# The opening of a two-layer decoder trunk: its first loads in 128 KB pieces, its first products in program order, and four matmuls of ones

## The chip, the cores and the metric

The kernel runs on one core of one Trainium2 chip. The metric is the device time of one execution in microseconds; the time before the change is 1127.63 us, the median of three runs (1126.76 to 1127.94). One further execution was recorded by the hardware profiler. Five engines work side by side, each through its own list of instructions in order: PE (TensorE: matmuls, with its weight loads shown as PEld), DVE (VectorE), ACT (ScalarE), POOL (GpSimd) and SP (SyncE), which here only issues DMAs.

## The reference

A trunk of two layers over 256 tokens of width 2048, in float32. Each layer normalises, projects, mixes tokens (layer 0: a gated linear recurrence beside an RG-LRU; layer 1: mLSTM), projects back, and then adds a gated embedding of its own:

```python
for i in range(DEPTH):
    hn = rmsnorm(h, e_norm[j] if i % 2 == 0 else o_norm[j])
    ...
    h = h + mix
    pl = rmsnorm(p[i].astype(h.dtype) @ ple_w[i], ple_norm[i])
    h = h + jax.nn.sigmoid(h @ ple_gate_w[i]) * pl
return rmsnorm(h, final_norm)
```

The change touches how `p[0] @ ple_w[0]` is started (a 256x256 matrix by a 256x2048 matrix). Nothing that is computed changes.

## The kernel before

**Numbers in two parts.** Every float32 operand of a large product is split into `hi` (the value rounded to a shorter float, type fp32r) and `lo` (what is left). A product is then three matmuls, hi x hi, hi x lo and lo x hi, summed in PSUM. So each weight that arrives from memory goes through two instructions: ACT writes `whi` (line 123), DVE subtracts and writes `wlo` (line 124). Activations go the same way (`split_act`, lines 138 and 139, tile `ahl`).

**Loading.** `load_weights` (lines 112 to 127) loads one block of 128 x 2048 weights (1 MB) as two halves of 512 KB into tiles `raw` (five buffers), `whi` and `wlo` (four buffers each). With `pieces=2` the first half comes as two transfers of 256 KB, each split as soon as it is there. All loads are issued by SP in program order. The splits are given a high priority (line 122), so the scheduler, which decides each engine's order when the program is built, places them early.

**The opening.** `load_p(0)` (line 321) loads the embedding input, 256 KB, as `praw` and splits it. `ple(0, ...)` (lines 326 to 345) then computes the embedding products: two blocks `b` of weights, four output tiles `j` in each, and for each tile two columns `jj` and two depths `k`. Each (jj, k) is one `mm3` (lines 142 to 145): hi x hi on line 143, hi x lo on line 144, lo x hi on line 145. That is 2 x 4 x 2 x 2 x 3 = 96 matmuls of 256 columns. Tiles j = 0 and 1 use the first half of the block's weights, j = 2 and 3 the second half. The results are copied out of PSUM by ACT (line 343) and DVE (line 341) in turn. The scheduler may interleave these matmuls between tiles as it likes.

**What follows.** The value projection `i_proj` (line 603) runs `project_tok` (lines 176 to 196) twice, 96 matmuls of 512 columns each time (lines 191 to 193). During the first, `load_x` (line 436) brings in the four pieces of `x`; DVE multiplies them by the norm gains (line 302, tile `hn`) and splits them, ACT squares them, and POOL adds the squares (line 285). When the sums are complete, `normed` (line 287) makes the normalised activations on DVE (line 292, again tile `hn`, then the split on lines 138 and 139). The first projection `f_proj` (line 521, matmuls on lines 154 and 160) needs all of them.

The instruction lists below are those of the programs as built.

Of the kernel before, what the change touches and what calls it, by code (L numbers as in the profile page):

```python
# [11 lines left out]
F32 = mybir.dt.float32  # L12
# [4 lines left out]
ALU = mybir.AluOpType  # L17
PSUM = bass.MemoryType.PSUM

P = 128  # L20
T = 256
# [24 lines left out]
def trunk(ctx: ExitStack, tc: tile.TileContext, a, out):  # L46
    nc = tc.nc
    v, s, gp, te, sy = nc.vector, nc.scalar, nc.gpsimd, nc.tensor, nc.sync
# [7 lines left out]
    px = ctx.enter_context(tc.tile_pool(name="px", bufs=3, space=PSUM))  # L56
# [5 lines left out]
    last = {}  # L62
# [27 lines left out]
    ones = cp.tile([P, T], F32, name="ones")  # L90
    gp.memset(ones, 1.0)
    eps = cp.tile([P, 1], F32, name="eps")
    gp.memset(eps, EPS)
    ident = cst[:, 0:128]
    c0 = 128
    lmask = {}
# [7 lines left out]
    def pc(name, i=0, n=None):  # L104
        o, w = PRM[name]
        return prm[:, o + i:o + i + (n or 1)]

    def pall(name):
        return pc(name, 0, PRM[name][1])


    def load_weights(src, pieces=1):
        parts = []
        for hf in range(2):
            raw = wp.tile([P, 1024], F32, name="raw", tag="raw", bufs=5)
            hi = wp.tile([P, 1024], F32R, name="whi", tag="whi")
            lo = wp.tile([P, 1024], F32R, name="wlo", tag="wlo")
            n = 1024 // pieces
            for c in range(0, 1024, n):
                r, h, l = (x[:, c:c + n] for x in (raw, hi, lo))  # L120
                sy.dma_start(out=r, in_=src[:, hf * 1024 + c:hf * 1024 + c + n])
                with tc.high_priority(offset=400):
                    last["act"] = s.copy(h, r).ins  # L123
                    last["dve"] = v.tensor_tensor(out=l, in0=r, in1=h.bitcast(F32), op=ALU.subtract).ins  # L124
            parts.append((hi, lo))
            pieces = 1
        return parts

    def act_pair():

        x = ap.tile([P, 1024], F32R, name="ahl", tag="ahl")
        x4 = x.rearrange("p (k i t) -> p k i t", i=2, k=2)
        return x4[:, :, 0], x4[:, :, 1], x

    def split_act(src, name):
        hi, lo, both = act_pair()
        src = src.rearrange("p (k t) -> p k t", k=2)
        s.copy(hi, src)  # L138
        v.tensor_tensor(out=lo, in0=src, in1=hi.bitcast(F32), op=ALU.subtract)  # L139
        return hi, lo, both  # L140

    def mm3(o, whi, wlo, x, k, first, end):
        te.matmul(o, whi, x[0][:, k], start=first, stop=False)  # L143
        te.matmul(o, whi, x[1][:, k], start=False, stop=False)  # L144
        last["pe"] = te.matmul(o, wlo, x[0][:, k], start=False, stop=end).ins  # L145

    def block(w, act):


        ps = pm.tile([P, 512], F32, name="mm", tag="mm")  # L150
        parts = load_weights(w)
        for k in range(KT):
            c = (k % 8) * P
            last["pe"] = te.matmul(ps, parts[k // 8][0][:, c:c + P],  # L154
                                   act[k // 2][2][:, (k % 2) * 512:(k % 2 + 1) * 512],
                                   start=(k == 0), stop=False).ins
        pump()
        for k in range(KT):
            c = (k % 8) * P
            last["pe"] = te.matmul(ps[:, T:2 * T], parts[k // 8][1][:, c:c + P], act[k // 2][0][:, k % 2],  # L160
                                   start=False, stop=(k == KT - 1)).ins
        return ps
# [6 lines left out]
    def project(w, pair, act, which=(0, 1)):  # L169

        m = tp.tile([P, 512], F32, name="mg", tag="hn", bufs=3)
        for j in which:
            merge(m[:, j * T:(j + 1) * T], block(w[2 * pair + j], act))
        return m

    def project_tok(w, j, act, before=None):

        ps = [pm.tile([P, 512], F32, name="mm", tag="mm") for _ in range(2)]
        for kq in range(4):
            if before is not None:  # L180
                before(kq)
            parts = load_weights(w[4 * j + kq])
            for hf in range(2):
                for kk in range(4):
                    k = kq * 4 + kk
                    hi, lo = parts[kk // 2]
                    c = (kk % 2) * 512
                    ah, al, _ = act[k // 2]
                    xh, xl = (x[:, k % 2, hf * P:(hf + 1) * P] for x in (ah, al))
                    wh, wl = hi[:, c:c + 512], lo[:, c:c + 512]  # L190
                    te.matmul(ps[hf], xh, wh, start=(k == 0), stop=False)  # L191
                    te.matmul(ps[hf], xh, wl, start=False, stop=False)  # L192
                    last["pe"] = te.matmul(ps[hf], xl, wh, start=False, stop=(k == KT - 1)).ins  # L193
                if hf == 0:
                    pump()
        return ps
# [123 lines left out]

    def load_p(i):
        praw = tp.tile([P, 512], F32, name="praw", tag="hn", bufs=3)
        sy.dma_start(out=praw, in_=a["pT"][i])
        return split_act(praw, "p")

    def ple(i, pact, pool, tag, between=None):
        pls = []
        for b in range(2):
            parts = load_weights(a["pw"][2 * i + b], 2 if i == b == 0 else 1)
            if b == 1 and between is not None:  # L330
                between()
            for j in range(4):
                hi, lo = parts[j // 2]
                pl = pool.tile([P, 512], F32, name="pl", tag=tag, bufs=10 if tag == "qk" else 8)
                ps = pm.tile([P, 512], F32, name="mm", tag="mm")
                for jj in range(2):
                    for k in range(2):
                        c = ((j % 2) * 4 + jj * 2 + k) * P
                        mm3(ps[:, jj * T:(jj + 1) * T], hi[:, c:c + P], lo[:, c:c + P], pact, k, k == 0, k == 1)
                if j % 2:  # L340
                    v.tensor_copy(pl, ps)
                else:
                    s.copy(pl, ps)
                pls.append(pl)
        return pls
# [76 lines left out]
    def small(n, name, rows=P):  # L422
        return cp.tile([rows, n], F32, name=name)
# [5 lines left out]
    m0_scope = ExitStack()  # L429
    m0 = m0_scope.enter_context(tc.tile_pool(name="m0", bufs=2))  # L430
    pls = ple(0, load_p(0), p0, "pl", lambda: sy.dma_start(out=prm, in_=a["prm"]))
    identr = cp.tile([8, 8], F32R, name="identr")
    acc = cp.tile([P, 512], F32, name="acc", tag="acc")
# [12 lines left out]
    pgh = []  # L446
    for i in range(2):
        t = small(16, f"pgh{i}")
        v.tensor_scalar(t, pall(f"pn{i}"), 0.5, None, op0=ALU.mult)
        pgh.append(t)  # L450

    norm = {}
# [1 line left out]
    def finish_norm(accs, hq, g, act, lag):  # L454
# [10 lines left out]
    act = []  # L465

    mx, e0, e1, lb, omb, sp, ez, z2, pol, sp8, spm8, anh = (small(8, n) for n in (
        "mx", "e0", "e1", "lb", "omb", "sp", "ez", "z2", "pol", "sp8", "spm8", "anh"))
# [41 lines left out]
    with m0_scope:  # L510
        ew = a["ew"]
        fs, qs, ks = [], [], []
        for g in range(2):
            f = m0.tile([P, 1024], F32, name="f", tag="f")
            k = m0.tile([P, 1024], F32, name="k", tag="k")
            q = m0.tile([P, 1024], F32, name="q", tag="q")
# [209 lines left out]
    for i in range(4):  # L726
        t = hp.tile([P, 1024], F32, name="hq", tag="h")
# [7 lines left out]
    act = []  # L735
# [3 lines left out]
    with tc.tile_pool(name="m1", bufs=2) as m1:  # L739
# [31 lines left out]
        ps = pm.tile([P, 512], F32, name="mm", tag="mm")  # L771
        for hf in range(2):
# [4 lines left out]
            for w in range(2):  # L777
                src = gr[:, hf * 8:(hf + 1) * 8, w * 8:(w + 1) * 8]
                c = w * 32
                s.copy(w3[:, :, c:c + 8], src)  # L780
                v.tensor_tensor(out=w3[:, :, 64 + c:72 + c], in0=src, in1=f3[:, :, c:c + 8], op=ALU.subtract)
            for kk in range(8):
                k = hf * 8 + kk
                for i, x in enumerate(act[k // 2][0:2]):
                    te.matmul(ps[:, 0:T], wt[:, kk * P:(kk + 1) * P], x[:, k % 2],  # L785
                              start=(k == i == 0), stop=(k == KT - 1 and i == 1))
# [131 lines left out]
        for j in range(8):  # L918
            ps = project(a["oog"], j, act)
# [5 lines left out]
            if j >= 3:  # L925
                for jj, t in held:
                    v.scalar_tensor_tensor(nums[jj], t, 1.0, nums[jj], op0=ALU.add, op1=ALU.mult)
                held = []
        pact = load_p(1)
        y = []  # L930
        for j in range(8):
            y.append(gate_split(a["oz"], j, lambda: nums[j], False))

        pls = ple(1, pact, m1, "qk")
        start("pl", ple_norm(1, pls))
        acc = cp.tile([P, 512], F32, name="acc", tag="acc")
        _, accs = finish_layer(hq, a["oo"], a["g1"], y, pls, acc, None)
# [3 lines left out]
        for k, n in ((0, 1), (1, 1), (12, 2), (2, 2), (4, 2), (14, 2), (6, 2), (8, 2), (10, 2)):  # L941
            hh = hq[k // 4][:, (k % 4) * T:(k % 4 + n) * T]
            eng, r = (gp, rs) if k >= 12 else (v, rsp)
# [105 lines left out]
```

## Time and profile before

| | |
|---|---|
| time, median of 3 runs | 1127.63 us (1126.76 to 1127.94) |
| the profiled execution | 1128.09 us |
| its span, first to last instruction | 1126.3 us |
| PE busy | 1098.4 us, 98% of the span |
| DVE busy | 807.5 us, 72% |
| ACT busy | 591.6 us, 53% |
| mean granted TensorE clock | 0.992 |

Times in the views are microseconds from the first instruction of the span. A row of the timeline gives start, duration, engine, line, operation, the tile written and the tiles read, the shape, the number of instructions merged, and in brackets how long the engine had been idle and what ended the idle time. SPq is SP's DMA queue: such a row is the issue of a transfer, not the transfer. A row of the table by windows gives for each stretch the busy time of each engine with its number of instructions, then the granted clock of TensorE, the busy share of the DMA engines, and GB/s.

### The profile page before, as it was taken

To read this page: it belongs to the slowest core of one execution; us is meant where nothing else is said; L and a number is where in the kernel's file an instruction comes from. 1 tells how busy PE (TensorE), PEld (TensorE's weight loads), DVE (VectorE), ACT (ScalarE), POOL (GpSimd) and SP (SyncE) were. 2 spreads that over 40 slices of the span, in tenths; PEclk is the share of its full clock that TensorE was granted. 3 is DMA by queue.
4 is the path that set the end of the run, shared out by engine and by line. 5 is a ranking of instruction groups with operands and counts; after the bars stand their busy time and mean duration, and the time that the engine had idled before them with its cause. 6 is when DMAs were issued, how large, how long until landed. Compare 5 with 4: busy or idle time off the path is not lost.

```text
span 1126.3 us, 16575 instructions
## 1 busy us (share of the span) xinstructions
PE 1098.4 (98%) x6298; PEld 953.9 (85%) x6298; DVE 807.5 (72%) x1197; ACT 591.6 (53%) x812; POOL 110.0 (10%) x80
## 2 busy tenths in 40 slices
PE   7999999999999999999999999999999989999995
PEld 6778898888888888888888888888888888888884
DVE  7998776798867656787745876659566568856775
ACT  6565435666645435555545655544455465435552
POOL 2144000000000000111000011110000013500111
PEclk9999999999999999999999999999999999999997
DMA  8655545443565555555555544444565555555642
GB/s 318 206 177 187 164 138 167 150 150 132 169 205 198 195 187 187 187 188 188 190 188 169 188 135 143 150 149 157 190 203 188 190 168 166 194 189 188 194 137 75
DMA packets 55519, 198.34 MB, mean 176 GB/s; under 512 B 6160, under 2 KB 6672, under 8 KB 55440
## 3 DMA queue, kind: packets, MB, share of 16 engines
q1 hardware_dynamic: 54864, 195.20, 52.2%
q0 software_dynamic: 576, 2.10, 0.6%
q8 instruction: 49, 0.80, 0.3%
q14 instruction: 30, 0.25, 0.1%
HBM read 195.17 MB, written 2.10 MB: 175 GB/s over the span
## 4 chain that ended last, share of the span: by engine, by line
PE 91%; DVE 1%; ACT 1%; issue 0%; POOL 0%; DVEq 0%; ACTq 0%; POOLq 0%
PE mm L154 49%; PE mm L160 26%; PE mm L191 2%; PE mm L193 2%; PE mm L192 2%; PE mx L572 2%; PE mx L875 1%; PE mx L670 1%; PE mm L143 0%; PE mm L144 0%; PE mx L264 0%; PE mm L145 0%; PE st L831 0%; PE mm L785 0%; PE st L631 0%
## 5 line engine op out<-in xcount | busy, mean ns | idle before, releaser
L124 DVE TENSOR_TENSOR wlo<-raw,whi 128x1024 fp32r<-128x1024 f32 (+1 forms) x361 | 456.7, 1300 | 205.0 <-issue 80.1
L154 PE MATMUL mm<-ahl,whi 128*128 128x512 f32 x2432 | 582.5, 392 | 2.3 <-DVE ahl L139 2.3
L123 ACT CAST whi<-raw 128x1024 fp32r<-128x1024 f32 (+1 forms) x361 | 376.5, 1046 | 296.1 <-PE mm L154 224.9
L154 PEld LDWEIGHTS mm<-ahl,whi 128*128 128x128 f32 x2432 | 446.7, 188 | 91.4 <-DVE ahl L139 4.4
L160 PE MATMUL mm<-ahl,wlo 128*128 128x256 f32 x2432 | 322.0, 286 | 0.0
L160 PEld LDWEIGHTS mm<-ahl,wlo 128*128 128x128 f32 x2432 | 310.7, 192 | 11.4 <-issue 1.3
L166 ACT COPY sm<-mm 128x256 f32<-128x256 f32 x120 | 44.4, 371 | 100.4 <-PE mm L160 100.0
L191 PE MATMUL mm<-whi,ahl 128*128 128x512 f32 x192 | 75.6, 394 | 0.1
L193 PE MATMUL mm<-whi,ahl 128*128 128x512 f32 x192 | 74.9, 391 | 0.2 <-DVE ahl L139 0.2
L192 PE MATMUL mm<-wlo,ahl 128*128 128x512 f32 x192 | 75.0, 390 | 0.0
L285 POOL TENSOR_TENSOR acc<-acc,sq 128x512 f32<-128x512 f32 x17 | 27.7, 1628 | 298.1 <-ACT sq L284 223.2
L167 DVE TENSOR_TENSOR mg<-mm,sm 128x256 f32<-128x256 f32 x120 | 50.0, 417 | 2.6 <-ACT sm L166 2.5
L193 PEld LDWEIGHTS mm<-whi,ahl 128*128 128x128 f32 x192 | 36.0, 188 | 8.4 <-DVE ahl L139 1.0
L191 PEld LDWEIGHTS mm<-whi,ahl 128*128 128x128 f32 x192 | 36.1, 188 | 8.1 <-ACT ahl L138 0.5
L192 PEld LDWEIGHTS mm<-wlo,ahl 128*128 128x128 f32 x192 | 36.1, 188 | 7.8 <-DVE wlo L124 0.5
L285 POOL TENSOR_TENSOR placc<-placc,sq 128x512 f32<-128x512 f32 x14 | 22.8, 1625 | 202.0 <-ACT sq L284 176.6
L365 POOL TENSOR_TENSOR pl<-pl,plrs 128x512 f32<-128x512 f32 x16 | 30.9, 1963 | 34.9 <-ACT plrs L276 34.9
L143 PE MATMUL mm<-ahl,whi 128*128 128x256 f32 x64 | 20.0, 313 | 10.8 <-ACT whi L123 7.7
L752 DVE SCALAR_TENSOR_TENSOR qk<-mg,prm,qk 128x255 f32<-128x255 f32 (+2 forms) x48 | 22.2, 479 | 11.6 <-ACT qk L749 11.0
L138 ACT CAST ahl<-hn 128x512 fp32r<-128x512 f32 x32 | 19.4, 616 | 15.9 <-DVE hn L292 9.9
L728 POOL DMA_DIRECT2D hq<-in_xT_dram x4 | 2.3, 578 | 235.1 <-PE mx L624 177.6
L143 PEld LDWEIGHTS mm<-ahl,whi 128*128 128x128 f32 x64 | 13.8, 216 | 11.3 <-ACT whi L123 8.0
(241 smaller groups left out, 777.5 us busy)
## 6 DMA issues: line engine op xcount, KB each, us to landing
raw<-in_ew_dram SPq DMA_DIRECT2D x80, 512.0 KB, 4.4
raw<-in_g_dram SPq DMA_DIRECT2D x64, 512.0 KB, 4.4
raw<-in_eo_dram SPq DMA_DIRECT2D x32, 512.0 KB, 4.8
raw<-in_ov_dram SPq DMA_DIRECT2D x32, 512.0 KB, 4.1
raw<-in_oqk_dram SPq DMA_DIRECT2D x32, 512.0 KB, 4.3
raw<-in_oog_dram SPq DMA_DIRECT2D x32, 512.0 KB, 4.2
raw<-in_oz_dram SPq DMA_DIRECT2D x32, 512.0 KB, 4.3
raw<-in_oo_dram SPq DMA_DIRECT2D x32, 512.0 KB, 4.3
```

Source lines behind the costliest of these rows:

```text
L123: last["act"] = s.copy(h, r).ins
L124: last["dve"] = v.tensor_tensor(out=l, in0=r, in1=h.bitcast(F32), op=ALU.subtract).ins
L143: te.matmul(o, whi, x[0][:, k], start=first, stop=False)
L154: last["pe"] = te.matmul(ps, parts[k // 8][0][:, c:c + P], act[k // 2][2][:, (k % 2) * 512:(k % 2 + 1) * 512], start=(k == 0), stop=False).ins
L160: last["pe"] = te.matmul(ps[:, T:2 * T], parts[k // 8][1][:, c:c + P], act[k // 2][0][:, k % 2], start=False, stop=(k == KT - 1)).ins
L166: s.copy(small, ps[:, T:2 * T])
L167: v.tensor_tensor(out=dst, in0=ps[:, 0:T], in1=small, op=ALU.add)
L191: te.matmul(ps[hf], xh, wh, start=(k == 0), stop=False)
L192: te.matmul(ps[hf], xh, wl, start=False, stop=False)
L193: last["pe"] = te.matmul(ps[hf], xl, wh, start=False, stop=(k == KT - 1)).ins
L285: eng.tensor_tensor(out=acc, in0=acc, in1=sq, op=ALU.add)
L365: gp.tensor_tensor(out=x3, in0=x3, in1=rs.unsqueeze(1).to_broadcast([P, 2, T]), op=ALU.mult)
```

## The change

- A PSUM tile `idle` is taken, and four float32 matmuls of ones by ones (128 x 256) are written into it before anything else; nothing reads it.
- `load_p(0)` loads its input as two transfers of 128 KB, the first issued by SP, the second by ACT, and splits each by itself.
- The first half of the first weight block comes in four pieces of 128 KB instead of two of 256 KB. The splits of these pieces and of the input are chained with `issue_after`, so ACT and DVE take them in this order: input part 0, weight piece 0, input part 1, weight pieces 1, 2, 3. Other weights keep the high priority.
- In `ple`, each `mm3` is chained behind the last PE instruction, so PE takes the embedding products in program order.
- The two small products `pgh` are chained behind the last DVE split.

```diff
+    idle = px.tile([P, 512], F32, name="mx", tag="mx")
+    for _ in range(4):
+        last["pe"] = te.matmul(idle[:, 0:T], ones[:, 0:P], ones, start=True, stop=True).ins
...
+    opening = []
...
-                with tc.high_priority(offset=400):
+                with ExitStack() as order:
+                    if pieces > 1:
+                        for ins in (last["act"], last["dve"]):
+                            order.enter_context(tc.issue_after(ins))
+                    else:
+                        order.enter_context(tc.high_priority(offset=400))
                     last["act"] = s.copy(h, r).ins
                     last["dve"] = v.tensor_tensor(out=l, in0=r, in1=h.bitcast(F32), op=ALU.subtract).ins
+                if opening:
+                    opening.pop()()
...
         praw = tp.tile([P, 512], F32, name="praw", tag="hn", bufs=3)
-        sy.dma_start(out=praw, in_=a["pT"][i])
-        return split_act(praw, "p")
+        if i:
+            sy.dma_start(out=praw, in_=a["pT"][i])
+            return split_act(praw, "p")
+        x = act_pair()
+
+        def part(k):
+            r = praw[:, k * T:(k + 1) * T]
+            with ExitStack() as order:
+                if k:
+                    for ins in (last["act"], last["dve"]):
+                        order.enter_context(tc.issue_after(ins))
+                last["act"] = s.copy(x[0][:, k], r).ins
+                last["dve"] = v.tensor_tensor(out=x[1][:, k], in0=r, in1=x[0][:, k].bitcast(F32),
+                                              op=ALU.subtract).ins
+
+        for k, q in enumerate((sy, s)):
+            q.dma_start(out=praw[:, k * T:(k + 1) * T], in_=a["pT"][i][:, k * T:(k + 1) * T])
+        part(0)
+        opening.append(lambda: part(1))
+        return x
...
-            parts = load_weights(a["pw"][2 * i + b], 2 if i == b == 0 else 1)
+            parts = load_weights(a["pw"][2 * i + b], 4 if i == b == 0 else 1)
...
-                        mm3(ps[:, jj * T:(jj + 1) * T], hi[:, c:c + P], lo[:, c:c + P], pact, k, k == 0, k == 1)
+                        with ExitStack() as behind:
+                            if "pe" in last:
+                                behind.enter_context(tc.issue_after(last["pe"]))
+                            mm3(ps[:, jj * T:(jj + 1) * T], hi[:, c:c + P], lo[:, c:c + P], pact, k, k == 0, k == 1)
...
-        v.tensor_scalar(t, pall(f"pn{i}"), 0.5, None, op0=ALU.mult)
+        with tc.issue_after(last["dve"]):
+            v.tensor_scalar(t, pall(f"pn{i}"), 0.5, None, op0=ALU.mult)
```

## The prediction

> **What bounds the kernel now.** I read four views: the page's engine line and chain, for the whole; the table by windows, for the first 75 us, the only stretch whose built order of instructions the change moves (PE's list is the same from its 334th instruction on, DVE's from its 151st); the timeline of the opening; and the timeline of PE's waits. The page first: busy time of each engine, and the chain of work that ended last by engine.
>
> ```profile
> PE 1098.4 (98%) x6298; PEld 953.9 (85%) x6298; DVE 807.5 (72%) x1197; ACT 591.6 (53%) x812; POOL 110.0 (10%) x80
> ...
> PE 91%; DVE 1%; ACT 1%; issue 0%; POOL 0%; DVEq 0%; ACTq 0%; POOLq 0%
> ```
>
> Over the whole span PE is the bound. That is an average. The windows tell another story for the start (stretch; busy time and count of PE, PEld, DVE, ACT, POOL; clock, DMA share, GB/s):
>
> ```profile
> 6.00:10.20 4.20, 2.45 (x9) 2.16 (x10) 1.39 (x2) 1.75 (x3) 0.00 (x0) 1.00 0.99 350
> 10.20:30.00 19.80, 19.65 (x124) 17.89 (x124) 19.59 (x27) 14.50 (x22) 8.31 (x5) 1.00 0.91 353
> 30.00:50.00 20.00, 19.83 (x88) 15.51 (x87) 19.83 (x69) 12.34 (x20) 1.34 (x2) 1.00 0.61 205
> 50.00:66.00 16.00, 16.00 (x72) 13.28 (x71) 15.51 (x27) 10.10 (x15) 0.00 (x0) 1.00 0.60 197
> 66.00:74.40 8.40, 6.06 (x24) 4.36 (x24) 8.40 (x8) 6.68 (x11) 4.23 (x3) 0.95 0.45 142
> ```
>
> From 10.2 to 74.4 us DVE is busy 19.59 + 19.83 + 15.51 + 8.40 = 63.3 of 64.2 us: it has no slack at all. PE is as full until 66 us and then idles. What it idles for:
>
> ```profile
> 71.61 0.73 PE L154 MATMUL mm<-ahl,whi 128*128 128x512 f32 x2 [1.33 <-DVE ahl L139]
> 73.35 1.12 PE L154 MATMUL mm<-ahl,whi 128*128 128x512 f32 x2 [1.01 <-DVE ahl L139]
> ```
>
> At 70.3 us (71.61 less 1.33) PE has caught up with DVE and waits for the last normalised activations. So in the first 75 us PE runs on time that DVE sets, and the question of this change is when DVE's unbroken stretch begins. The opening:
>
> ```profile
> 0.74 1.28 ACT L138 ACT_TABLE_LOAD   x1 [0.74 <-PEq L1040]
> 0.74 0.31 POOL L91 MEMSET ones<- 128x256 f32 x1 [0.29 <-POOLq L1040]
> 0.74 0.38 SPq L323 DMA_DIRECT2D praw<-in_pT_dram  x1
> ...
> 1.18 2.32 SPq L121 DMA_DIRECT2D raw<-in_pw_dram  x5
> 3.47 0.62 ACT L138 CAST ahl<-praw 128x512 fp32r<-128x512 f32 x1 [1.45 <-DMA praw<-in_pT_dram]
> ...
> 5.49 0.62 ACT L123 CAST whi<-raw 128x512 fp32r<-128x512 f32 x1 [1.40 <-DMA raw<-in_pw_dram]
> ...
> 6.16 0.58 PE L143 MATMUL mm<-ahl,whi 128*128 128x256 f32 x1 [6.16 <-ACT whi L123]
> ...
> 7.88 0.62 ACT L123 CAST whi<-raw 128x512 fp32r<-128x512 f32 x1 [1.77 <-DMA raw<-in_pw_dram]
> ...
> 8.55 0.58 PE L143 MATMUL mm<-ahl,whi 128*128 128x256 f32 x1 [1.59 <-ACT whi L123]
> ...
> 9.17 1.04 ACT L123 CAST whi<-raw 128x1024 fp32r<-128x1024 f32 x1 [0.68 <-DMA raw<-in_pw_dram]
> ...
> 10.25 2.51 DVE L124 TENSOR_TENSOR wlo<-raw,whi 128x1024 fp32r<-128x1024 f32 x2 [1.03 <-ACT whi L123]
> ```
>
> DVE's stretch begins at 10.25 with the split of the block's second half (call it H), behind ACT's cast at 9.17, behind H's landing. The two 256 KB pieces came at 5.49 and 7.88.
>
> **The change part by part.** The sum is made against the profiled execution, 1128.09 us (span 1126.3, so 1.8 us lie around it); the median of the runs, 1127.63, is 0.46 lower.
>
> *Four matmuls of ones.* A float32 matmul of 256 columns is two records; the trace has one at half clock and one at full:
>
> ```profile
> 47.89 0.60 PE L248 MATMUL st<-dg,ones 128*128 128x256 f32 x2
> ...
> 1116.01 1.19 PE L248 MATMUL st<-dg,ones 128*128 128x256 f32 x2 [2.09 <-DVE dg L245]
> ```
>
> They can start when the ones are written, 0.74 + 0.31 = 1.05. Four take between 4 x 0.60 = 2.4 and 4 x 1.19 = 4.8 us; nothing has run before, so I take the upper end: until 5.8 at most. Today's first weights are cast at 5.49, so they can hold up the first product by 0.3 us, which (below) has cover. Cost 0.
>
> *The loads.* SP's issues stand 2.32 / 5 = 0.46 us apart. H is today the third of the five, issued at 1.18 + 2 x 0.46 = 2.1; afterwards the input's part and four pieces stand before it: 0.74 + 0.44 + 4 x 0.47 = 3.1, almost a microsecond later. The bytes ahead of it stay 768 KB. How long such a transfer is under way, from the view of tile raw in the first 25 us, and the rate once the queue is full:
>
> ```profile
> DMA to landing us min/median/max: 4.3/7.8/9.7
> ...
> 14.00:20.00 6.00, 6.00 (x53) 6.00 (x51) 5.98 (x10) 4.65 (x8) 1.41 (x1) 1.00 1.03 409
> ```
>
> The trace has no transfer of 128 KB, so H's landing is bounded: at the earliest 3.1 + 4.3 = 7.4, which is 1.8 before today's 9.17; at the latest today's plus the whole later issue, 10.1, 0.9 after. Today H is 7 us under way (2.1 to its cast at 9.17), so bytes and stragglers set it, not its issue: the second piece came 2.39 us after the first, though 256 KB take 0.64 at 409 GB/s. I take 0.4 earlier, near today's row, because part of that straggling may go when the pieces are small. ACT's own issue costs at most the 0.46 of SP's; with the 1.28 of the table load ACT is free at 2.5, before the 3.47 at which the input comes today. SP's next loads go out two issues later into a queue that is full anyway. Cost 0.
>
> *Smaller splits.* Six casts instead of three on ACT, six subtractions instead of three on DVE. ACT has 1.40 and 1.77 us of idle time ahead of its casts and DVE 1.03 ahead of H: hidden, unless the last piece comes less than a microsecond before H.
>
> *Program order of the products.* Their spacing, before and after the clock rises:
>
> ```profile
> 10.21 0.41 PE L145 MATMUL mm<-ahl,wlo 128*128 128x256 f32 x1
> 10.42 0.41 PE L143 MATMUL mm<-ahl,whi 128*128 128x256 f32 x1
> ...
> 21.32 0.28 PE L145 MATMUL mm<-ahl,wlo 128*128 128x256 f32 x1
> 21.44 0.40 PE L191 MATMUL mm<-whi,ahl 128*128 128x512 f32 x1
> ```
>
> 0.21 us cold, 0.12 warm. The first two tiles need 24 products and only the pieces: from 5.8 that ends at 8.7 warm or 10.9 cold. The third tile needs H's low part, which DVE has at 10.25 + 2.51 / 2 = 11.5; its third matmul waits for it, and in program order all later ones are queued behind. So whether the ones warm the clock hardly matters: PE stands at 11.5 in either case. From there 70 products x 0.12 = 8.4 give 19.9 instead of 21.44. **PE gains 1.5 us here.**
>
> *And loses it.* DVE's list from H on holds the same instructions. A copy out of PSUM (line 341) moves up between H and the next split and waits for PE's second tile, done by 10.9, before DVE gets there: no stall. So DVE ends its stretch when it did, moved only by H, and PE, 1.5 us early, waits 1.5 us more at 70 us. Net 0. What is left is H's 0.4.
>
> *POOL beside DVE.* DVE's end also hangs on collisions with POOL's additions:
>
> ```profile
> 50.29 1.67 DVE L292 SCALAR_TENSOR_TENSOR hn<-xq,prm,hrs 128x256 f32<-128x256 f32 x4
> ...
> 66.21 3.02 POOL L285 TENSOR_TENSOR placc<-placc,sq 128x512 f32<-128x512 f32 x2 [24.73 <-PE mm L193]
> 66.53 4.43 DVE L292 SCALAR_TENSOR_TENSOR hn<-xq,prm,hrs 128x256 f32<-128x256 f32 x3
> ```
>
> Four of these take 1.67; beside POOL three take 4.43 where 1.25 were due, 3.2 lost to two or three additions, 1.1 to 1.6 each. The additions stay; a few DVE instructions change places, so one collision more or less is possible: 0, within 1.1 either way.
>
> *The clock at 73.6.* The stall at 70 us has a second price:
>
> ```profile
> 70.20:73.60 3.40, 1.06 (x4) 0.55 (x4) 3.40 (x5) 2.61 (x4) 0.47 (x1) 0.98 0.02 6
> 73.60:77.00 3.40, 3.40 (x16) 3.21 (x16) 1.56 (x2) 3.09 (x5) 2.17 (x2) 0.52 0.84 242
> ```
>
> After 3.4 us in which PE worked only 1.06, the next 3.4 ran at half clock: 16 matmuls at 0.21 instead of 0.12, 1.5 us at most. The stall gets longer, so I expect this again: 0; if it stays away, 1.5 less. The Trainium skill (TensorE: Matmul & The Clock Gate, Part 1, "What's actually happening") halves the clock after an idle window of some 3.4 us on a free-running grid. The length agrees; but this window held 1.06 us of work, so "idle" is too strict here. By the page's word no half clock would follow a window with work, and the sum would be 1.5 lower.
>
> Sum: 1128.09 + 0 (ones) - 0.4 (H) - 1.5 + 1.5 (PE early, then waiting) + 0 (POOL) + 0 (clock) = 1127.7, or **1127.2 us** beside the median.
>
> **The rivals.**
>
> *H lands early* (faster). For it: stragglers, not bytes, delay H today, and 4.3 us under way occurs. Against it: its bytes and its place in the queue stay. Price: 1.8 from the bound, and up to 1.5 if the shifted stall misses the slow clock: 1124.3 to 1125.8, say 1125.0. The Trainium skill (DMA: Bandwidth & Descriptors, "Anatomy of one DMA") gives 2.0 us plus bytes at 436 GB/s; by that, an estimate, H would land at 3.1 + 2.0 + 1.2 = 6.3 and save 2.9. The trace does not agree: the second 256 KB took from an issue at 1.6 to their cast at 7.88.
>
> *H lands late* (slower). If each piece straggles as today's second does (2.39 - 0.64 = 1.75 lost) and there are two pieces more, H comes 3.5 later, DVE starts 3.5 later, and nothing downstream gives it back: 1131.1. It decides once H lands after 11.4 (2.25 us later). Against it: the later rows of the queue run at 409 GB/s without such gaps.
>
> *The slow clock stays away at 73.6*, with H as forecast: 1127.2 - 1.5 = 1125.7.
>
> *The ones do not warm the clock.* Then the first 24 products take 5.1 us instead of 2.9, and PE still waits for H: the same time, part of the forecast.
>
> **How the numbers follow.** Forecast 0.55, slow clock away 0.15, H early 0.2, H late 0.1. About 0.2% (2.25 us) is what a measurement of this kernel can tell from no change; the first two cases lie within it, so faster 0.2, same 0.7, slower 0.1. The range takes in H's upper bound with part of a POOL collision (1127.2 + 1.3 + 0.4 = 1128.9) and, below, half of the early case: 1125.2 to 1128.9.
>
> **What would show it.** In the changed profile: ACT's cast of H near 8.8 and DVE busy without a break from there; the first product of line 191's loop near 19.5 to 20; PE's waits for ahl between 28 and 74 us longer by about 1.5 in sum; half clock somewhere between 70 and 78. The forecast is wrong if H is cast before 7.5 or after 11, if DVE idles between 15 and 70, or if PE does not wait near 70 us.

## The result, and the profile after

The changed kernel took 1131.24 us (median of nine runs, 1129.2 to 1133.24 but for one of 1362.0, which the ratio leaves out), the kernel before in the same comparison 1127.94: a ratio of 1.0027, 95% interval 1.0018 to 1.0036. It is 3 us slower; 1127.2, in a range up to 1128.9, had been forecast. The profiled execution spans 1128.8 us, 2.5 more than before. In the fences below, line numbers are those of the kernel named: in the changed kernel line 133 is ACT's `whi`, 134 DVE's `wlo`, 150 and 151 the split into `ahl`, 155 to 157 the embedding products, 203 to 205 the loop products (191 to 193 before), 296 and 297 the squares and their addition, 374 and 376 the copies out of PSUM; other edits shift them by a few.

The changed kernel's page, engines and chain:

```profile
PE 1102.4 (98%) x6306; PEld 954.9 (85%) x6306; DVE 806.3 (71%) x1200; ACT 592.1 (52%) x815; POOL 114.9 (10%) x80
...
PE 91%; DVE 4%; issue 1%; ACT 1%; POOL 1%; DMA 1%; SPq 0%; DVEq 0%; ACTq 0%; POOLq 0%
```

DVE has 4% of the chain where it had 1%. Where, the table by windows of the changed kernel shows (same columns and stretches as in the prediction):

```profile
6.00:10.20 4.20, 2.21 (x17) 1.84 (x15) 0.78 (x3) 1.64 (x4) 0.00 (x0) 1.00 0.94 334
10.20:30.00 19.80, 18.51 (x104) 15.97 (x105) 17.20 (x28) 14.14 (x21) 5.86 (x4) 0.91 0.91 344
30.00:50.00 20.00, 17.55 (x74) 13.14 (x74) 17.63 (x49) 10.63 (x17) 7.98 (x3) 1.00 0.58 187
50.00:66.00 16.00, 15.96 (x71) 12.91 (x70) 15.56 (x42) 8.97 (x14) 0.00 (x0) 1.00 0.63 201
66.00:74.40 8.40, 8.40 (x38) 6.64 (x36) 8.40 (x10) 7.57 (x13) 4.34 (x3) 1.00 0.53 178
```

From 10.2 to 50 us DVE is busy 17.20 + 17.63 = 34.83 us instead of 39.42. It was to have no slack, and now it stands still for 4.6 us more. The opening, from the changed kernel's timeline of 0 to 12.2 us:

```profile
1.10 3.78 PE L96 MATMUL mx<-ones 128*128 128x256 f32 x8 [1.10 <-POOL eps L93]
...
4.32 0.78 PE L155 MATMUL mm<-ahl,whi 128*128 128x256 f32 x1
...
9.11 1.04 ACT L133 CAST whi<-raw 128x1024 fp32r<-128x1024 f32 x1 [2.56 <-DMA raw<-in_pw_dram]
...
10.21 0.39 PE L155 MATMUL mm<-ahl,whi 128*128 128x256 f32 x1 [2.00 <-ACT whi L133]
...
11.46 0.39 PE L157 MATMUL mm<-ahl,wlo 128*128 128x256 f32 x1 [0.76 <-DVE wlo L134]
```

The pieces do come early: the first product starts at 4.32 instead of 6.16, and two tiles are done when PE begins to wait at 8.2. But H, the block's second half, is cast at 9.11 as before (9.17). Into PE's wait falls the next event, in the windows of the changed kernel (granted clock third from the end):

```profile
8.20:12.00 3.80, 1.05 (x7) 0.83 (x7) 1.81 (x3) 2.77 (x4) 0.00 (x0) 1.00 0.99 381
12.00:15.40 3.40, 3.40 (x18) 3.40 (x17) 2.28 (x3) 2.38 (x4) 0.11 (x1) 0.50 1.02 410
...
73.60:77.00 3.40, 1.65 (x8) 1.04 (x7) 3.40 (x5) 3.40 (x6) 0.24 (x2) 1.00 0.13 39
```

After 3.8 us with 1.05 us of matmuls the clock halves from 12.0 to 15.4, and PE's gain is gone: the loop of line 203 begins at 21.45, where it began at 21.44 before. The time is lost in what follows. DVE, POOL and ACT of the changed kernel, from its timelines of 14.5 to 20 and of 27 to 40.5 us:

```profile
15.90 0.69 DVE L374 COPY pl<-mm 128x512 f32<-128x512 f32 x1 [1.62 <-PE mm L157]
...
18.77 0.69 DVE L374 COPY pl<-mm 128x512 f32<-128x512 f32 x1 [0.98 <-PE mm L157]
```

```profile
28.54 1.21 DVE L134 TENSOR_TENSOR wlo<-raw,whi 128x1024 fp32r<-128x1024 f32 x1
28.55 8.77 POOL L297 TENSOR_TENSOR acc<-acc,sq 128x512 f32<-128x512 f32 x2 [3.35 <-ACT sq L296]
...
34.54 1.28 DVE L512 TENSOR_TENSOR e<-prm,mx 128x8 f32<-128x8 f32 x1
...
35.83 0.63 ACT L296 ACTIVATE sq<-xq 128x512 f32<-128x512 f32 x1 [3.43 <-POOL acc L297]
37.35 0.63 ACT L296 ACTIVATE sq<-xq 128x512 f32<-128x512 f32 x1 [0.88 <-POOL acc L297]
37.35 0.69 DVE L297 TENSOR_TENSOR acc<-acc,sq 128x512 f32<-128x512 f32 x1 [1.19 <-POOL acc L297]
37.89 1.03 ACT L133 CAST whi<-raw 128x1024 fp32r<-128x1024 f32 x1
...
38.95 1.22 DVE L134 TENSOR_TENSOR wlo<-raw,whi 128x1024 fp32r<-128x1024 f32 x1 [0.91 <-ACT whi L133]
```

Two things are to be seen. DVE waits 1.62 and 0.98 us for the products that it is to copy, and PE was at half clock until 15.4; before, DVE took the same copies at 15.88 and 18.76, without a wait. So PE's products came no earlier than before, and DVE came too early for them. And of two POOL additions that take 8.77 us together, the first holds ACT's next square until 35.8, 7.3 us after its start; before, the same two took

```profile
26.34 3.79 POOL L285 TENSOR_TENSOR acc<-acc,sq 128x512 f32<-128x512 f32 x2 [1.48 <-ACT sq L284]
```

The square stands in ACT's list ahead of the `whi` at 37.89, so DVE waits for POOL (1.19) and then for ACT (0.91). PE pays for it in the loop of line 203; the view of waits of the changed kernel, 25 to 45 us (waiter, what it waited for: sum, times, longest):

```profile
ACT sq L296 <- POOL acc L297: 4.3, 2, 3.4
...
PE mm L203 <- ACT ahl L150: 2.1, 2, 1.8
```

DVE's time can be added up. From H's split to the first normalised activation (`hn<-xq,prm,hrs`) both kernels have the same 96 DVE instructions. "Stretched" is what instructions took beyond their undisturbed length (`identr`: 1.25 instead of 0.15) beside POOL's five additions of x's squares; "idle" counts gaps of over 0.1 us. All is read from DVE's timelines:

| kernel | H's split | first `hn` with `hrs` | between | DVE idle in it | stretched by the additions |
|---|---|---|---|---|---|
| before | 10.25 | 50.29 | 40.04 | 0 | 4.19 |
| changed | 10.19 | 53.97 | 43.78 | 4.87 | 2.75 |
| changed, profiled again | 9.09 | 52.84 | 43.75 | 3.67 | 3.85 |

So 3.74 us more in the first pair: 4.87 of waiting (1.62 + 0.98 + 1.19 + 0.91 + 0.17) less 1.44 of stretching. The other 0.3 is overlap: in the trace a DVE instruction often starts a little before the one ahead of it has ended, 6.59 us in sum before and 6.26 in the changed kernel, where the waits break the row.

### The profile page after: what moved, and what is told of

Same layout as the page of the kernel before. It is cut to its first block, busy times and chain, and to the rows that moved or that the text cites. A ratio compares the mean times of both kernels' runs of the same rounds, so it can differ in the third digit from the quotient of the medians.

```text
span 1128.8 us, 16605 instructions
## 1 busy us (share of the span) xinstructions
PE 1102.4 (98%) x6306; PEld 954.9 (85%) x6306; DVE 806.3 (71%) x1200; ACT 592.1 (52%) x815; POOL 114.9 (10%) x80
## 4 chain that ended last, share of the span: by engine, by line
PE 91%; DVE 4%; issue 1%; ACT 1%; POOL 1%; DMA 1%; SPq 0%; DVEq 0%; ACTq 0%; POOLq 0%
PE mm L166 49%; PE mm L172 26%; PE mm L203 3%; PE mm L205 3%; PE mm L204 3%; PE mx L606 2%; DVE wlo L134 1%; DVE ahl L151 1%; POOL acc L297 1%; PE mx L909 1%; PE mx L704 1%; DMA raw<-in_pw_dram 1%; PE mm L157 1%; PE mm L155 1%; PE mm L156 1%
## 5 line engine op out<-in xcount | busy, mean ns | idle before, releaser
L166 PEld LDWEIGHTS mm<-ahl,whi 128*128 128x128 f32 x2432 | 446.3, 188 | 92.1 <-DVE ahl L151 4.7
L297 POOL TENSOR_TENSOR acc<-acc,sq 128x512 f32<-128x512 f32 x17 | 32.3, 1901 | 300.7 <-ACT sq L296 225.8
L151 DVE TENSOR_TENSOR ahl<-hn,ahl 128x512 fp32r<-128x512 f32 x32 | 24.1, 767 | 0.0
```

The source lines that it names most:

```text
L166: last["pe"] = te.matmul(ps, parts[k // 8][0][:, c:c + P], act[k // 2][2][:, (k % 2) * 512:(k % 2 + 1) * 512], start=(k == 0), stop=False).ins
L297: eng.tensor_tensor(out=acc, in0=acc, in1=sq, op=ALU.add)
```

## The experiments

The ratios are to the kernel before, run in the same comparison; each experiment had 5 rounds.

| run | median us | ratio, 95% interval |
|---|---|---|
| changed kernel | 1131.24 | 1.0027 (1.0018 to 1.0036) |
| changed kernel again | 1130.03 | 1.0021 (1.0011 to 1.0031) |
| program order alone | 1127.58 | 0.9995 (0.9986 to 1.0004) |
| pieces and fixed order alone | 1129.34 | 1.0012 (1.0003 to 1.0021) |
| ones alone | 1135.38 | 1.0053 (1.0036 to 1.0070) |
| changed, without ones | 1128.61 | 1.0005 (0.9996 to 1.0014) |
| changed, one of the ones, 256 columns | 1129.28 | 1.0015 (1.0006 to 1.0024) |
| changed, one of the ones, 128 columns | 1128.80 | 1.0011 (1.0002 to 1.0020) |
| changed, ones in PE's wait too | 1128.84 | 1.0008 (0.9999 to 1.0017) |
| changed, four buffers for squares | 1128.74 | 1.0008 (0.9999 to 1.0017) |
| changed, x's additions on DVE | 1127.92 | 0.9997 (0.9989 to 1.0006) |
| changed, no ones, x's additions on DVE | 1128.21 | 1.0001 (0.9992 to 1.0010) |
| before, x's additions on DVE | 1127.22 | 0.9992 (0.9983 to 1.0001) |
| program order, x's additions on DVE | 1126.90 | 0.9992 (0.9983 to 1.0001) |
| program order, all 12 additions on DVE | 1123.96 | 0.9962 (0.9950 to 0.9975) |
| changed, all 12 additions on DVE | 1123.56 | 0.9960 (0.9948 to 0.9973) |

**Theory**: the 3 us come from a new order of ACT's and DVE's instructions, in which a POOL addition is held back and ACT's squares behind it hold up casts. **Rivals**: the clock that halves in PE's wait; program order; the transfers in pieces.

**Program order alone** (kernel before):

```diff
-                        mm3(ps[:, jj * T:(jj + 1) * T], hi[:, c:c + P], lo[:, c:c + P], pact, k, k == 0, k == 1)
+                        with ExitStack() as behind:
+                            if "pe" in last:
+                                behind.enter_context(tc.issue_after(last["pe"]))
+                            mm3(ps[:, jj * T:(jj + 1) * T], hi[:, c:c + P], lo[:, c:c + P], pact, k, k == 0, k == 1)
```

> The kernel before, with one part of the change alone: every embedding product is chained behind the last PE instruction. ACT's list stays as it was, and DVE's first 60 instructions too. Theory (the 3 us come from the new order of ACT's and DVE's instructions between 10 and 50 us, in which a POOL addition is held back and ACT's squares behind it hold up casts): no change, within 0.6 us of the kernel before. Rival, program order itself (each tile's copy out of PSUM waits for all products ahead of it): 1.5 to 3 us slower.

No change, as the theory had it. Its DVE timeline shows what became of an early start: H's split began at 9.27, 0.98 earlier than in the kernel before, and DVE's list is the same up to its 61st instruction.

```profile
13.57 2.19 DVE L302 TENSOR_SCALAR hn<-xq,prm 128x256 f32<-128x256 f32 x4
...
19.75 1.78 DVE L139 TENSOR_TENSOR ahl<-hn,ahl 128x512 fp32r<-128x512 f32 x1
21.45 1.24 DVE L476 CAST identr<-cst 8x8 fp32r<-8x8 f32 x1
...
27.13 1.78 DVE L139 TENSOR_TENSOR ahl<-hn,ahl 128x512 fp32r<-128x512 f32 x1
28.83 2.17 DVE L302 TENSOR_SCALAR hn<-xq,prm 128x256 f32<-128x256 f32 x4
```

Four gains take 1.14 undisturbed, an `ahl` 0.68, this cast 0.15: each of the five POOL additions stretches one DVE instruction by 1.1 us. In the kernel before the five cost 0.43, 0.49, 1.10, 1.10 and 1.07, 4.2 us. So the early start is lost by 27 us, and the first `hn` with `hrs` comes at 50.04 instead of 50.29. What POOL's additions cost DVE depends on where they meet it.

**Pieces and fixed order alone** (the changed kernel without its ones and without the chaining of `mm3`):

```diff
-    idle = px.tile([P, 512], F32, name="mx", tag="mx")
-    for _ in range(4):
-        last["pe"] = te.matmul(idle[:, 0:T], ones[:, 0:P], ones, start=True, stop=True).ins
...
-                            if "pe" in last:
-                                behind.enter_context(tc.issue_after(last["pe"]))
```

> The kernel before, with the four 128 KB pieces, the split input, their fixed order and the chained pgh, but without ones and without program order of the products. From the four hn gains on, ACT's and DVE's lists have the pairs that the changed kernel has (two ahl splits together, two squares together). Theory (order of the lists): 2 to 4 us slower than the kernel before, with a POOL addition of over 6 us between 25 and 40 us. Rival, the cold clock: without ones the clock rises once, near 11 to 12, as before, and there is no second half-clock window at 12: no loss, within 0.6 us. Rival, the transfers (two more DMAs, one on ACT's queue, xq and later weights issued later): 2 to 4 us slower too, but with weights or xq late in the waits and no long POOL addition.

Slower, by less than I had said (1.4 us). POOL is held back here too, without any second half clock; its timeline and DVE's:

```profile
19.43 12.00 POOL L294 TENSOR_TENSOR acc<-acc,sq 128x512 f32<-128x512 f32 x4 [3.92 <-ACT sq L293]
...
30.30 2.21 DVE L131 TENSOR_TENSOR wlo<-raw,whi 128x1024 fp32r<-128x1024 f32 x1 [2.79 <-ACT whi L130]
```

**Ones in PE's wait too** (behind tile 1 of the first block) and **four buffers for x's squares** (changed kernel):

```diff
+                if i == b == 0 and j == 1:
+                    with tc.issue_after(last["pe"]):
+                        for _ in range(4):
+                            last["pe"] = te.matmul(idle[:, 0:T], ones[:, 0:P], ones, start=True, stop=True).ins
```

```diff
-            add_square(gp if j < 6 else v, acc, pair_of(xq, j), j == 0)
+            add_square(gp if j < 6 else v, acc, pair_of(xq, j), j == 0, ("sq", "th")[j % 2])
```

> The changed kernel, with four more matmuls of ones behind the second tile's products, so that PE works through 8.2 to 10.6 us where it waits for the block's second half. Rival, the cold clock (the half-clock window at 12.0 to 15.4 is what puts the copies and then everything late): no half clock at 12, copies on time, 3 us faster than the changed kernel or more (1126 to 1128). Theory (order of the lists): here the scheduler also happens to put ACT's and DVE's instructions near the order of the kernel before (ahl and whi in turn), so it expects 3 us faster as well, with no POOL addition over 5 us; if the clock stays full but a POOL addition is still held for 7 us, it expects at most 1.5 faster.

> The changed kernel with the squares of x written in turn to two tags (sq and th, which nothing else uses then), four buffers instead of two. The built order of ACT and DVE is the same, instruction for instruction. Theory: a held-back POOL addition no longer stops ACT's next squares, so the waits of ACT at 32 to 38 us (3.43 and 0.88 for POOL) go, whi and ahl come on time, and 2 to 3 us of the 3 come back (1128 to 1129). Rival, the cold clock, and rival, the transfers: no more than 0.6 us faster than the changed kernel.

Both are 1.5 to 2 us below the changed kernel by their ratios, and near the one before. The first had no half clock at 12 and no long addition, so it separates nothing. The second kept the lists, and the same two additions took 8.77 us again, from 26.88. ACT no longer waited for POOL at all, and of the waits behind the addition only DVE's own one of 1.19 us was left:

```profile
35.68 0.69 DVE L297 TENSOR_TENSOR acc<-acc,sq 128x512 f32<-128x512 f32 x1 [1.19 <-POOL acc L297]
```

DVE needed 41.73 us from H's split to its first `hn` with `hrs`, 2 less than the changed kernel. But its profile had no half clock at 12 either (full from 6.87). Against the run below that has the same lists and no half clock (one matmul of ones, 256 columns: 42.30), the buffers are worth 0.6.

**The changed kernel again**, and **x's additions on DVE** in it:

```diff
-            add_square(gp if j < 6 else v, acc, pair_of(xq, j), j == 0)
+            add_square(v, acc, pair_of(xq, j), j == 0)
```

> The changed kernel itself once more, unedited, as a control for the others of this comparison and for the phase of the clock. In the four profiles so far TensorE's full clock began at 5.17, 6.67, 6.87 and 7.89 us without any edit that would set it. Theory now (two causes: where the clock's 3.4 us windows happen to fall against PE's wait at 8.2 to 10.2 us, and the POOL addition that is held back): the median stays 1130 to 1132, and if in this profile no half-clock window follows at 10 to 15 us, DVE's waits for PE at 15.9 (1.62) and 18.8 (0.98) are gone while POOL's addition of over 6 us is still there, and PE at 50 us is 1.3 to 2.5 us late against the kernel before instead of 4.1. Rival (order of the lists alone): the waits at 15.9 and 18.8 are there in any case.

> The changed kernel with the five additions of x's squares that POOL did done by DVE instead. They add 5 x 0.61 to 0.69 = 3.1 to 3.5 us to DVE. Theory: they take away what POOL's additions cost DVE in the changed kernel, 2.75 us by which DVE instructions were stretched and 1.19 + 0.91 of waiting: 0.4 to 1.8 us faster than the changed kernel, and no wait of ACT for POOL. Rival (POOL's additions are off the path, DVE has no slack): 3 us slower than the changed kernel, 1134.

The repeat gave what the two-cause reading expects, and one thing more. The program is the same, but H was cast a microsecond earlier (8.02), PE's wait was shorter, and no half clock follows it:

```profile
8.20:12.00 3.80, 2.33 (x17) 1.93 (x16) 2.67 (x3) 3.02 (x4) 0.00 (x0) 1.00 1.01 387
12.00:15.40 3.40, 3.40 (x31) 3.40 (x30) 3.32 (x5) 2.71 (x6) 1.17 (x1) 1.00 1.02 406
```

The copies came on time and the loop began at about 18.9. The additions at 26.28 took 8.77 again. But here the clock halved later, behind PE's wait for an activation, and DVE waited for a product there. From the PE timeline, the windows and the DVE timeline of this profile:

```profile
42.31 0.50 PE L203 MATMUL mm<-whi,ahl 128*128 128x512 f32 x1 [1.79 <-ACT ahl L150]
```

```profile
42.77:46.18 3.41, 3.41 (x11) 2.66 (x10) 2.25 (x9) 1.04 (x1) 0.74 (x1) 0.50 0.91 269
```

```profile
46.38 0.38 DVE L241 TENSOR_SCALAR rsv<-st 128x1 f32<-128x1 f32 x2 [1.32 <-PE st L237]
```

So DVE's stretch was as long as in the first profile (43.75 and 43.78), and its first `hn` with `hrs` came 2.55 late instead of 3.68 because H came 1.1 earlier. These two profiles don't separate the half clock from POOL's hold.

With the five additions on DVE the loss is gone: 1127.92 beside 1130.03 in the same comparison, with intervals that don't meet, although this profile has the half clock at 11.7 to 15.1 and DVE's waits for the copies (1.30 and 0.69). DVE does 5 x 0.61 to 0.69 us more, and the kernel is faster by it. The edit also lets the scheduler reorder DVE's and ACT's other instructions, so the time alone doesn't single out POOL; in the trace no instruction of the stretch is lengthened but one, by 0.44 (beside the addition with which POOL folds the finished sums, `acc<-acc`), and between 10 and 55 us no engine waits for POOL.

**Ones alone** (kernel before):

```diff
+    idle = px.tile([P, 512], F32, name="mx", tag="mx")
+    for _ in range(4):
+        last["pe"] = te.matmul(idle[:, 0:T], ones[:, 0:P], ones, start=True, stop=True).ins
```

> The kernel before with the four matmuls of ones alone. DVE's and ACT's lists from 10 us on change with it, into the pairs of the changed kernel (two ahl splits together, all of one x piece's gains together). Theory (order of the lists): a POOL addition of over 6 us between 25 and 40 us and 1 to 3 us slower than the kernel before. Rival (ones only warm the clock): the first products at 0.12 instead of 0.21 us and no more than 0.6 us of difference either way.

The slowest of all, more than I expected; its six runs lie between 1130.6 and 1136.5. An early full clock without early pieces: PE has nothing to do, and the clock halves again and again. From its windows:

```profile
5.80:9.20 3.40, 0.80 (x6) 0.68 (x6) 0.69 (x1) 0.62 (x1) 0.00 (x0) 1.00 0.95 350
9.20:12.60 3.40, 3.40 (x18) 3.40 (x17) 1.22 (x1) 2.71 (x4) 0.00 (x0) 0.50 1.03 385
...
43.40:46.80 3.40, 3.40 (x9) 2.67 (x8) 3.40 (x8) 0.69 (x2) 3.11 (x1) 0.50 0.69 218
77.50:84.30 6.80, 5.35 (x22) 4.62 (x21) 3.72 (x3) 2.49 (x5) 4.75 (x4) 0.50 0.36 128
```

Its lists have the pairs of the changed kernel, and two additions took 8.77 us from 28.25. How much of its loss is the clock's and how much the lists', this run doesn't separate.

**Without ones**, and with **one matmul of ones** of 256 or of 128 columns (changed kernel):

```diff
-    for _ in range(4):
-        last["pe"] = te.matmul(idle[:, 0:T], ones[:, 0:P], ones, start=True, stop=True).ins
+    for _ in range(1):
+        last["pe"] = te.matmul(idle[:, 0:256], ones[:, 0:P], ones[:, 0:256], start=True, stop=True).ins
```

> The changed kernel without the four matmuls of ones. ACT's and DVE's lists are then those of the run with the pieces alone (1129.34). Theory: the ones bring nothing here (the clock is full before 8 us without them too) and only stretch PE's wait and reorder the lists: 1128.5 to 1130, 0.5 to 2 us faster than the changed kernel. Rival (the ones warm the clock and that pays): slower than the changed kernel, 1131 to 1133, with the first full clock after 10 us.

> The changed kernel with one matmul of ones (256 columns) instead of four. The lists of all five engines stay those of the changed kernel, instruction for instruction, but for the three matmuls that are left out; PE has at most 1.2 us of ones instead of 3.8. Theory A (the lists cost): as slow as the changed kernel, 1130 to 1131.5, with a POOL addition of some 7 us between 25 and 40 us and ACT's and DVE's waits behind it. Theory B (the clock, warm too early by the ones, halves in PE's wait): 1128 to 1129, as without ones, with no half clock at 12.

> The same with the one matmul of ones of 128 columns. PE's work differs by about half a microsecond from that with 256 columns, at the very start, but the lists of all engines become those of the changed kernel without ones. Theory A (the lists cost): 1.5 to 2.5 us faster than with 256 columns, as without ones (1128.6). Theory B (the clock): the same time as with 256 columns, within 0.6.

Without ones the time is the one forecast (1128.61) and within noise of the kernel before. One matmul of 256 columns keeps the lists of ACT, DVE and POOL, one of 128 gives those without ones. The two are 0.0004 apart, and the first lies between what the two theories expected: neither list is the dear one. Both hold POOL back, the first kernel's timeline and the second's:

```profile
27.28 8.77 POOL L297 TENSOR_TENSOR acc<-acc,sq 128x512 f32<-128x512 f32 x2 [3.35 <-ACT sq L296]
```

```profile
21.34 11.65 POOL L297 TENSOR_TENSOR acc<-acc,sq 128x512 f32<-128x512 f32 x4 [4.22 <-ACT sq L296]
```

So the narrower form of my theory, that the list made by the ones is to blame, falls. With fewer ones the medians are 1 to 2 us lower, but the intervals of one and of four ones overlap: that the ones themselves cost is likely, not shown.

The run with 256 columns also sizes the two causes, since it has the changed kernel's lists and full clock from 8.77 until long after the stretch. Its DVE timeline:

```profile
10.41 1.23 DVE L134 TENSOR_TENSOR wlo<-raw,whi 128x1024 fp32r<-128x1024 f32 x1 [2.87 <-ACT whi L133]
...
36.08 0.69 DVE L297 TENSOR_TENSOR acc<-acc,sq 128x512 f32<-128x512 f32 x1 [1.19 <-POOL acc L297]
37.68 1.23 DVE L134 TENSOR_TENSOR wlo<-raw,whi 128x1024 fp32r<-128x1024 f32 x1 [0.91 <-ACT whi L133]
...
52.71 1.67 DVE L304 SCALAR_TENSOR_TENSOR hn<-xq,prm,hrs 128x256 f32<-128x256 f32 x4
```

DVE took 42.30 us between the two ends. That is 2.3 more than before, with the two waits behind POOL's addition and three others, of 0.17 us at most; the changed kernel's 43.78 is 1.5 more again, with the half clock. So, one profile each, of 3.7 us about 2.3 go to the lists with POOL's hold and 1.5 to the half clock.

**x's additions on DVE** without the change, with program order, and with the change less its ones:

> The kernel before with x's five additions on DVE and nothing else. In its trace the five POOL additions stretch DVE's instructions by 0.43 + 0.49 + 1.1 + 1.1 + 1.07 = 4.2 us; on DVE they take 3.1 to 3.5. Theory: 0.7 to 1.1 us faster than the kernel before, 1126.8 to 1127.2. Rival (DVE has no slack, POOL is free): 3 us slower, 1131.

> The kernel before with program order of the embedding products (which by itself made DVE's stretch begin 0.98 us earlier and lost it again to stretched DVE instructions) and with the five additions of x's squares on DVE. Theory: each POOL addition stretches a DVE instruction by about 1.1 us (5.9 us in sum with program order, five of them near 1.1), DVE itself needs 0.61 to 0.69 for one, so 5.5 - 3.3 = 2.2 us less: 1125 to 1126 where before has 1127.9. Rival (DVE has no slack and POOL is free): 3 us slower, 1131.

> The changed kernel without ones and with x's five additions on DVE. Theory: with H early, no POOL addition under DVE's stretch and no wait of DVE for PE's copies, DVE's 101 instructions from H on take 35.4 + 3.3 = 38.7 us plus idle: 1126 to 1127.5. Rival (the transfers in pieces cost something of their own): 1128 to 1130, not faster than the kernel before.

None is 3 us up, so POOL's additions are not free. The first gained 0.9 us in the median, as forecast, the second 1.0 where 2.2 were expected; both intervals just reach no change. The third gained nothing beside the kernel before, which is what its rival had (the pieces cost something of their own); the last run below speaks against that rival. Beside the first, the changed kernel with the same edit is 0.6 us slower by the ratios, where with POOL's additions it was 2.4 to 3.0. With program order no DVE instruction was stretched before 50 us but the one beside POOL's fold; then DVE waits for PE's chain to `hrs`, and POOL's next additions take the rest, as its DVE and PE timelines show:

```profile
49.62 1.67 DVE L292 SCALAR_TENSOR_TENSOR hn<-xq,prm,hrs 128x256 f32<-128x256 f32 x4 [1.36 <-ACT hrs L276]
...
63.75 5.62 DVE L292 SCALAR_TENSOR_TENSOR hn<-xq,prm,hrs 128x256 f32<-128x256 f32 x6
```

```profile
71.16 4.83 PE L154 MATMUL mm<-ahl,whi 128*128 128x512 f32 x13 [2.92 <-DVE ahl L139]
```

Six of these take 2.5 undisturbed (four take 1.67): 3.1 us lost, and PE waits 2.92.

**All 12 additions on DVE** (those of `placc` too), with program order and with the change:

```diff
-            add_square(gp, acc, pl, j == 0)
+            add_square(v if i == 0 else gp, acc, pl, j == 0)
```

> The kernel with program order and x's additions on DVE, and the seven additions of layer 0's embedding squares (placc, 66 to 82 us) on DVE too. In the kernel before, POOL's first additions there stretched three of DVE's hn instructions by 3.2 us just where PE waits for them. Theory: only two of the seven come ahead of DVE's last normalised activation, 2 x 0.65 = 1.3 instead of about 3.2: 1 to 2 us faster than with x's additions alone, 1125 to 1126. Rival (by 70 us PE or the clock's half window takes the gain): within 0.5 us of 1126.9.

> The changed kernel with all twelve of the opening's additions of squares (five of x, seven of placc) on DVE. Theory: with POOL's additions out of the way the change neither gains nor loses much against the kernel with program order and the same additions on DVE (1123.96): 1123.5 to 1125.5. Rival (the pieces, the ones or the fixed order cost something of their own): 1126 or more.

Both beat both kernels, the one before by 4 us in their own comparisons, which is more than expected of the first and as expected of the second. In the first one's DVE timeline of 60 to 78 us nothing is stretched, and its window of 66 to 74.4 has PE full:

```profile
64.54 1.66 DVE L292 SCALAR_TENSOR_TENSOR hn<-xq,prm,hrs 128x256 f32<-128x256 f32 x4
...
70.40 1.40 DVE L285 TENSOR_TENSOR placc<-placc,sq 128x512 f32<-128x512 f32 x2
```

```profile
66.00:74.40 8.40, 8.40 (x43) 6.87 (x42) 7.87 (x13) 7.77 (x12) 0.00 (x0) 1.00 0.57 186
```

And with or without the rest of the change the time is the same (0.9960 and 0.9962): the pieces, the fixed order of the splits and the ones neither cost nor gain what these runs can tell once POOL is out of DVE's way.

## Why the prediction was wrong, point by point

- *The step that failed* is "DVE's list from H on holds the same instructions ... So DVE ends its stretch when it did". The first half is right, 96 instructions in each; their order was not the same, and the time of a list depends on its order. DVE stood for 4.87 us in a stretch that had no idle time before. The prediction's own sign of being wrong, "if DVE idles between 15 and 70", came true.
- "*POOL beside DVE: 0, within 1.1 either way*" is the term that was mis-sized. I priced only DVE instructions that POOL stretches. Those became fewer (2.75 us instead of 4.19). What I left out is the other side: POOL held back by DVE, and behind POOL's addition ACT's squares, the casts and DVE again, 2.1 us of waiting. Taking x's additions off POOL took away 2.1 us in the same comparison.
- "*Whether the ones warm the clock hardly matters*": it did. The first 24 products ended at 8.2, near the 8.7 worked out for a warm clock, and the third tile did wait for H's low part (11.46, forecast 11.5). But the clock halved behind that wait, and 16 of the 70 products after it ran at 0.21 instead of 0.12. "No stall" held for the copy that it was said of (11.33, no wait), but the sum has no term for the next two, at which DVE stood 1.62 and 0.98. Beside the run with the same lists and no half clock (42.30 against 43.78), the clock is about 1.5 of the 3.7 us.
- "*PE gains 1.5 us here. And loses it*" was right as a mechanism, and is seen without disturbance with program order alone: the loop begins at 19.38 there and nothing comes of it. In the changed kernel the gain was lost before 21.45.
- *H, 0.4 earlier*: 0.06 in the first profile and 1.16 in the second of the same program. Over the kernels H's split began between 9.09 and 10.41, also where its transfers were not edited (9.15 to 10.31). The term is smaller than its scatter; neither rival on H was the case. The 6.3 us that the first of them takes from the Trainium skill (DMA: Bandwidth & Descriptors, "Anatomy of one DMA") goes by a fit that the section gives for transfers issued by GpSimd; H is issued by SP, and was cast at 9.11 and 8.02.
- *The clock at 73.6*: expected again, it stayed away. The granted clock is 1.00 from 73.6 to 77.0; PE's stall came at 74.4, with 1.65 us of matmuls in that window, where the window ahead of the half clock had 1.06 before. Where the first of the same matmuls ran at half clock before, 73.6 to 77.0, PE of the changed kernel made up about 1 us.
- The slower rival named had the right time (1131.1) and the wrong cause; that its number fits is luck.

The Trainium skill (SBUF — State Buffer, "Who interferes with whom") says that where DVE and GpSimd contend (as with two SBUF inputs on DVE's side against a GpSimd instruction that reads SBUF), whichever issues first gets the shared port pair for the whole instruction and the other blocks fully. The trace agrees for DVE: `e` at 34.54, an instruction of 0.15 us, takes 1.28 and ends where the addition does, at 35.8. For POOL it shows more: the addition at 28.55 began 0.01 after a DVE instruction and was let through not behind that one but some 6 us and a dozen DVE instructions later, when this `e` was stretched.

What stays open: why POOL gets in between two DVE instructions in one place and not in another; and how much of the gain from moving the additions is POOL's absence and how much the new order that comes with it.

## What to carry to other kernels

A full engine's time is its list in its order, with what other engines do to it: before costing a reordering at nothing, look for small work on a neighbouring engine that gets in its way, as POOL's additions do here, and for what is queued behind that work. An addition that POOL does "for free" cost DVE up to 1.1 us here, where DVE itself does it in 0.61 to 0.69. Starting earlier was worth nothing here, and the clock halved in the wait that it made (1.05 us of matmuls in 3.80), since the piece of data that the next wait hung on came no earlier.

## What was not expected of the hardware

- One POOL addition, 1.3 us undisturbed, ran 7.3 us under a DVE list without gaps. In five profiles (the changed kernel's two among them) the same pair took 8.77, in three with the other list four took 11.65 to 12.00.
- 1.05 us of matmuls in 3.80 us did not keep the clock up, 2.33 did. Over all 17 profiles, after the first full clock, the 3.41 us ahead of a half-clock stretch held between 0.01 and 2.32 us of matmuls, while no stretch of 3.41 us on the same grid with under 1.54 was followed by full clock; between the two both happened.
- The first full clock began between 4.87 and 13.26 us over the profiles, at 5.17 and 5.22 in two of one program. A half-clock stretch is 3.41 us long, or twice that, but for the last, in which the program ends.
- ACT's cast of the same 512 KB (H), which waits for their landing, began between 8.02 and 9.33 us in the eleven profiles with the transfers in pieces, and 1.09 apart in the two of one program.
